# The down projection of an encoder layer: one direct pair of K-tiles instead of two ahead of the seven-product form

## The chip, the cores and the metric

The kernel runs on one core of a Trainium2 chip. The metric is device time in microseconds, from the start to the end of one execution; smaller is better. The time before is the median of three runs.

## The reference, cut to what matters

The layer works on 512 tokens of width 2048 in float32. The part that the change touches is the last matrix product of the feed-forward block, with `w_down` of 5632 x 2048:

```python
h = rmsnorm(x, ffn_norm_w[l])
x = x + (jax.nn.silu(h @ w_gate[l]) * (h @ w_up[l])) @ w_down[l]
...
return rmsnorm(x, final_norm_w)
```

Before it stand the input projection, two kinds of attention and the output projection.

## The kernel before

Every float32 product is made of three matmuls in a shorter float type: each operand is split into a high part (a cast on ScalarE) and a low part (the difference, on VectorE), and high times high, high times low and low times high are summed in PSUM. The five engines run lists of instructions whose order is written out by hand; each engine works its list strictly in order. A list entry that waits holds everything behind it on that engine.

The 5632 rows of `w_down` are 44 K-tiles of 128, or 22 pairs. A column is one of four blocks of 512 output columns. Pairs are multiplied in one of two forms:

- **Direct** (`job` kind "B", run by `run_job`, L268; matmuls L304 to L306). For one pair and one column there are two half pieces of weights (`Stream.split`, cast L198, difference L199), each used on four token blocks with three matmuls 512 wide: 24 matmuls. The activations' operands come from `g_split` (L1303 to L1307 and its other branch).
- **Seven-product form** (class `Down`, L1358, on top of `Blocks`, L1121). A pair is a 2 x 2 block product done with seven products instead of eight. For one pair and one column: three sums of weights on VectorE (`sums`, L1157 to L1159), their and the weights' high parts (`split`, L1170, two casts) and low parts (L1175, two differences of 768 and 1024 columns), and 7 products x 2 token halves x 3 matmuls 256 wide (L1455 to L1457): 42 matmuls. For one pair once, a set of activations' operands is made (`operands`, L1379): four sums (L1402 to L1405), then four casts and four differences (L1414 to L1418). `make(n)` takes n steps of that generator: step one issues loads, and then each pair takes three steps (sums; the first two splits; the last two). `operands` loads a pair's activations from the scratch tensor `gd`.

The order of the stages is: gate/up (class `Feed`, L1181, in seven-product form, matmuls L1216 to L1218, 44 units of four pieces); the direct pairs 0 and 1 of `w_down`, column by column; `Down` with sixteen pairs in three chunks (2 to 7, 8 to 12, 13 to 17), each chunk through all columns; the pairs 18 and 19 direct (`later_jobs`); the pairs 20 and 21 direct, with the final norm (`finish`).

Around the joint of gate/up and the direct stage:

- `Feed.run` calls `down_start(q)` after each of the four pieces of the last unit, which begins loads and the first splits of the direct stage.
- The PSUM banks of a gate/up unit are read out by `Feed.evac` (L1222), a generator in the list `urgent`: its first step frees the unit's first bank (L1227, L1235), the second two banks, the third the last one. `run_urgent` takes one step. `run_side`, which calls it, stands in `run_job` behind every half piece but the last of a job: three times per column with four half pieces.
- There are eight PSUM banks of 512 columns. A column of the direct stage takes four from the front of the free list and returns them in `evac_down` (L1329): ScalarE scales each bank into SBUF (L1334), and GpSimd adds it to the scratch tensor `xd` by a DMA (L1336).
- `before_down(c)` runs ahead of every half piece of the direct stage, and steps the operands of `Down`, its first sums and its first split.
- The buffers `s4` (16 slots of 4 KB per partition, names b) hold raw weights and their splits, `s2` (70 slots of 2 KB, names a) the rest. SyncE issues the loads in program order and waits at a load until its slot is free.

Of the kernel before, what the change touches and what calls it, by code (L numbers as in the profile page):

```python
# [117 lines left out]
def layer(nc, tc, x, attn_norm_w, w_in, rel_table, gw_f, gb_f, gw_b, gb_b, gla_norm_w, w_out,  # L118
# [3 lines left out]
    w_gate, w_up, w_down, out = w_gate[0], w_up[0], w_down[0], out[0]  # L122
# [3 lines left out]
    with tc.manual_schedule(), \  # L126
# [6 lines left out]
        s4 = Slots(p4, N4, 1024, "b")  # L133
# [978 lines left out]
        for c in range(4):  # L1112
            j = job("B", [piece512(w_out, c * 512, k) for k in range(0, KT, 2)], list(range(KT)),
                    lambda k: mixh[k], evac_out(c), rate=1.0, start=start_out(c), before=before_out(c), limit=3)
# [176 lines left out]
        def g_load(j):  # L1291
            if j < FF // 256 and j not in graw and 2 * j not in gT and j >= state["g"]:
                state["g"] = j + 1
                graw[j] = s4.get(F32, [P, 2, 512])
                sp.dma_start(out=graw[j].t.rearrange("p f t -> p (f t)"), in_=gd[j])

        def g_split(j):
            if j in graw:
                r = graw.pop(j)
                for f in (1, 0):  # L1300
                    hi, lo = s2.get(F32R), s2.get(F32R)
                    if f:
                        act.activation(hi.t, r.t[:, f], AF.Copy, scale=-1.0)  # L1303
                        dve.scalar_tensor_tensor(lo.t, r.t[:, f], -1.0, hi.f, op0=OP.mult, op1=OP.subtract)
                    else:
                        act.copy(hi.t, r.t[:, f])
                        dve.tensor_tensor(lo.t, r.t[:, f], hi.f, op=OP.subtract)  # L1307
                    gT[2 * j + 1 - f] = (hi, lo)
                put(r)

        def down_start(q):
            if q == 0:
                g_load(0)
            if q == 1:
                st.until = down_pieces
                st.limit = 3
                st.load()
                g_load(1)
            if q == 2:
                g_split(0)  # L1320
                st.split(down_first + 2)
            if q == 3:
                dn.make(1)

        def residual(c, t, bank):
            dve.scalar_tensor_tensor(x1[c][t].t, bank.t, rstd2[:, t:t + 1], x1[c][t].t, op0=OP.mult, op1=OP.add)
# [12 lines left out]

        def before_down(c):  # L1340
            def f(i):
                if c == 0 and i == 0:
                    g_split(1)
                dn.make(1)
                if c == 3:
                    dn.load()
                    if i >= 1:
                        dn.sums(i - 1)
                    if i == 2:
                        dn.split(0)  # L1350
            return f

# [5 lines left out]
        class Down(Blocks):  # L1358
# [5 lines left out]
            def __init__(self, chunks):  # L1364
                self.chunks = chunks
                self.end = len(chunks) - 1
                cols = lambda ch: range(3, -1, -1) if ch % 2 else range(4)
                self.begin([(ch, c, q) for ch in range(len(chunks)) for c in cols(ch) for q in chunks[ch]], 1, 256)
                self.x = {}
                self.making = self.operands()  # L1370
                self.late = []
                self.stored = set()
                self.m, self.y = {}, {}
                self.ops = deque()
# [4 lines left out]
            def operands(self):  # L1379
                a, z = slice(0, 256), slice(256, 512)  # L1380
                tt = dve.tensor_tensor
                qs = deque(q for ch in self.chunks for q in ch)
                raws = deque()

                def load():
                    if qs and len(s4.free) > 1 and len(raws) < 2:
                        r = s4.get(F32, [P, 2, 512])
                        sp.dma_start(out=r.t.rearrange("p f t -> p (f t)"), in_=gd[qs[0]])
                        raws.append((qs.popleft(), r))

                load()
                load()
                yield
                while raws or qs:
                    load()
                    if not raws or len(s2.free) < 9 + 1:
                        yield
                        continue
                    q, r = raws.popleft()
                    n1, f2 = r.t[:, 1], r.t[:, 0]  # L1400
                    t13, t24 = s2.get(), s2.get()
                    tt(t13.t[:, a], n1[:, z], n1[:, a], op=OP.subtract)  # L1402
                    tt(t13.t[:, z], f2[:, z], n1[:, z], op=OP.add)
                    tt(t24.t[:, a], f2[:, z], t13.t[:, a], op=OP.add)
                    tt(t24.t[:, z], t24.t[:, a], f2[:, a], op=OP.subtract)  # L1405
                    yield
                    todo, slots = [], []
                    for src, n in ((n1[:, a], 256), (f2, 512), (t13.t, 512), (t24.t, 512)):
                        sl, hi, lo, hf = half_split(src, n)
                        slots += sl  # L1410
                        todo.append((src, hi, lo, hf))
                    for i, (src, hi, lo, hf) in enumerate(todo):
                        if i == 0:
                            act.activation(hi, src, AF.Copy, scale=-1.0)  # L1414
                            dve.scalar_tensor_tensor(lo, src, -1.0, hf, op0=OP.mult, op1=OP.subtract)
                        else:
                            act.copy(hi, src)
                            tt(lo, src, hf, op=OP.subtract)  # L1418
                        if i:
                            put((r, t13, t24)[i - 1])  # L1420
                        if i == 1:
                            load()
                        if i % 2:
                            yield
                    (_, b1h, b1l, _), (_, f2h, f2l, _), (_, t13h, t13l, _), (_, t24h, t24l, _) = todo
                    self.x[q] = dict(slots=slots, B11=(b1h, b1l), B21=(f2h[:, a], f2l[:, a]),
                                     B22=(f2h[:, z], f2l[:, z]), T1=(t13h[:, a], t13l[:, a]),
                                     T3=(t13h[:, z], t13l[:, z]), T2=(t24h[:, a], t24l[:, a]),
                                     T4=(t24h[:, z], t24l[:, z]))
# [104 lines left out]
            def run(self):  # L1534
                for i, (ch, c, q) in enumerate(self.seq):
                    self.load()
                    self.sums(i)
                    self.split(i)
                    self.sums(i + 1)
                    self.sums(i + 2)  # L1540
                    self.split(i + 1)
                    self.evac_late(i)
                    while q not in self.x:
                        self.make(1)
                    self.products(i)
                    if c == (0 if ch % 2 else 3) or i % 3:
                        self.make(1)
                    run_urgent()
                    if ch == self.end:
                        n = self.chunks[ch].index(q)  # L1550
                        self.combine(i, 2)
                        if c == 2 and n:
                            self.fetch(3, range(2 * n - 2, min(2 * n, 7)), sp)
                        if c == 3:
                            if n == 0:
                                g_load(LAST // 2 - 2)
                            if n == 1:
                                st.until, st.limit = None, 1
                                st.load()
                            if n == 2:  # L1560
                                g_split(LAST // 2 - 2)
                                g_load(LAST // 2 - 1)
                                st.limit = 2
                                st.load()
                            if n > 2:
                                st.split(later_first + n - 2)
                self.evac_late(len(self.seq))
                st.limit, st.big = 3, tail_first
# [26 lines left out]
        st.until = len(st.pieces)  # L1595
        down_first = len(st.halves)
        for c in range(4):
            j = job("B", [piece512(w_down, c * 512, k) for k in (0, 2)], list(range(4)),
                    lambda k: gT[k], evac_down(c), before=before_down(c))
            if c == 3:  # L1600
                j.drop = drop_g
# [9 lines left out]
            if c == 3:  # L1611
                j.drop = drop_g
        tail_first = len(st.halves)
        dn = Down([list(range(2, 8)), list(range(8, 13)), list(range(13, 18))])

        wf = []

# [127 lines left out]
```

## Time and profile before

| what | value |
|---|---|
| median of three runs | 2215.56 us (2215.52 to 2216.87) |
| the profiled execution's own time | 2216.53 us |
| its span, first to last instruction | 2214.8 us |
| granted TensorE clock, mean | 0.999 |
| busy: TensorE, VectorE, ScalarE, GpSimd | 2204.3, 1623.5, 1003.0, 96.0 us |
| matmuls | 14842 |

Durations in a timeline are those of one instruction until its result stands; the next one on the same engine may start some 0.1 us before that. So the price of an instruction in a chain is taken here from start to start. TensorE's line names its weight loads (PEld) apart from its matmuls (PE).

### The profile page before, as it was taken

What the parts mean: (1) busy time and instruction counts of PE and PEld (TensorE: products, weight loads), DVE (VectorE), ACT (ScalarE), POOL (GpSimd) and SP (SyncE); (2) the same over time, 40 slices, a digit from 0 to 9 for tenths busy, and PEclk for the clock granted to TensorE, in tenths of its full rate; (3) what the DMA queues carried; (4) which work ended last, traced back from release to release, by engine and by line L of the source; (5) the groups of instructions that cost most, each with busy time, mean ns of one, the idle gap of its engine ahead of it and who ended that gap; (6) DMA issues with size and microseconds to landing.
All of it is one profiled execution on the core that took longest, in us unless ns stands there. A gap on an engine that the chain in (4) does not pass through costs nothing.

```text
span 2214.8 us, 37040 instructions
## 1 busy us (share of the span) xinstructions
PE 2204.3 (100%) x14842; PEld 2040.1 (92%) x14842; DVE 1623.5 (73%) x2740; ACT 1003.0 (45%) x1664; POOL 96.0 (4%) x149
## 2 busy tenths in 40 slices
PE   9999999999999999999999999999999999999998
PEld 7888888888888888999999999999999999999987
DVE  4366665745454438988888888888888888888795
ACT  5244444444444345444434343444343465565462
POOL 0000000000000100000000000000000010011300
PEclk9999999999999999999999999999999999999999
DMA  6525625231324332334334333343333775575982
GB/s 207 162 82 158 169 87 141 76 124 57 96 67 153 131 127 77 115 115 124 115 115 124 115 124 115 115 125 115 115 125 115 249 164 179 167 195 143 288 316 76
DMA packets 210185, 302.26 MB, mean 136 GB/s; under 512 B 15005, under 2 KB 133197, under 8 KB 210014
## 3 DMA queue, kind: packets, MB, share of 16 engines
q1 hardware_dynamic: 194366, 258.87, 37.3%
q0 software_dynamic: 15328, 40.51, 7.2%
q8 instruction: 116, 1.90, 0.4%
q10 hardware_dynamic: 320, 0.53, 0.1%
q14 instruction: 55, 0.45, 0.1%
HBM read 246.58 MB, written 40.70 MB: 130 GB/s over the span
## 4 chain that ended last, share of the span: by engine, by line
PE 99%; DVE 1%; DMA 0%; SPq 0%; ACT 0%; issue 0%; DVEq 0%
PE ps L1217 13%; PE ps L1216 13%; PE ps L1218 13%; PE ps L304 7%; PE ps L306 7%; PE ps L305 7%; PE ps L297 5%; PE ps L295 5%; PE ps L296 5%; PE ps L1457 5%; PE ps L1456 5%; PE ps L1455 5%; PE ps L532 1%; PE ps L872 1%; PE ps L541 1%; PE ps L540 1%
## 5 line engine op out<-in xcount | busy, mean ns | idle before, releaser
L1216 PE MATMUL ps<-a,b 128*128 128x256 f32 x2464 | 697.5, 283 | 0.0
L1217 PE MATMUL ps<-a,b 128*128 128x256 f32 x2464 | 697.3, 283 | 0.0
L1218 PE MATMUL ps<-a,b 128*128 128x256 f32 x2464 | 697.3, 283 | 0.0
L1170 ACT CAST b<-b 128x1024 fp32r<-128x1024 f32 (+1 forms) x473 | 438.7, 941 | 529.1 <-DVE b L1175 280.6
L1175 DVE TENSOR_TENSOR b<-b,b 128x1024 fp32r<-128x1024 f32 (+1 forms) x473 | 501.5, 1087 | 123.3 <-PE ps L1217 61.6
L1217 PEld LDWEIGHTS ps<-a,b 128*128 128x128 f32 x2464 | 473.1, 192 | 0.0
L1216 PEld LDWEIGHTS ps<-a,b 128*128 128x128 f32 x2464 | 473.1, 192 | 0.0
L1218 PEld LDWEIGHTS ps<-a,b 128*128 128x128 f32 x2464 | 473.1, 192 | 0.0
L199 DVE TENSOR_TENSOR a<-b,a 128x512 fp32r<-128x512 f32 x292 | 194.7, 686 | 132.6 <-ACT a L198 121.5
L1456 PE MATMUL ps<-b,a 128*128 128x256 f32 x896 | 253.6, 283 | 0.0
L1457 PE MATMUL ps<-b,a 128*128 128x256 f32 x896 | 253.6, 283 | 0.0
L1455 PE MATMUL ps<-b,a 128*128 128x256 f32 x896 | 253.6, 283 | 0.0
L198 ACT CAST a<-b 128x512 fp32r<-128x512 f32 x292 | 170.8, 618 | 31.9 <-DMA b<-in_w_in_dram 10.9
L304 PE MATMUL ps<-a,a 128*128 128x512 f32 x464 | 182.7, 394 | 0.0
L305 PE MATMUL ps<-a,a 128*128 128x512 f32 x464 | 180.8, 390 | 0.0
L306 PE MATMUL ps<-a,a 128*128 128x512 f32 x464 | 180.7, 390 | 0.0
L1455 PEld LDWEIGHTS ps<-b,a 128*128 128x128 f32 x896 | 172.0, 192 | 0.0
L1456 PEld LDWEIGHTS ps<-b,a 128*128 128x128 f32 x896 | 172.0, 192 | 0.0
L1457 PEld LDWEIGHTS ps<-b,a 128*128 128x128 f32 x896 | 172.0, 192 | 0.0
L1157 DVE TENSOR_TENSOR b<-b 128x512 f32<-128x512 f32 x233 | 159.5, 684 | 10.8 <-DMA b<-in_w_down_dram 10.8
L295 PE MATMUL ps<-a,a 128*128 128x512 f32 x416 | 167.3, 402 | 0.0
L297 PE MATMUL ps<-a,a 128*128 128x512 f32 x416 | 163.0, 392 | 0.1
(240 smaller groups left out, 3059.7 us busy)
## 6 DMA issues: line engine op xcount, KB each, us to landing
b<-in_w_gate_dram SPq DMA_DIRECT2D x88, 512.0 KB, 3.5
b<-in_w_up_dram SPq DMA_DIRECT2D x88, 512.0 KB, 3.9
b<-in_w_down_dram SPq DMA_DIRECT2D x88, 512.0 KB, 4.9
b<-in_w_in_dram SPq DMA_DIRECT2D x48, 512.0 KB, 4.0
b<-in_w_in_dram SPq DMA_DIRECT2D x92, 256.0 KB, 4.4
b<-in_w_out_dram SPq DMA_DIRECT2D x32, 512.0 KB, 5.5
a<-a SPq DMA_DIRECT2D x96, 128.0 KB, 2.3
gd<-b POOLq DMA_DIRECT2D x22, 512.0 KB, 3.2
```

The costliest lines, as they stand in the source:

```text
L295: mm(o, wh.t[:, c], xh.t, start=first, stop=False)
L304: mm(o, xh.t[:, c], wh.t[:, w], start=first and not on, stop=False, skip_group_check=on)
L305: mm(o, xh.t[:, c], wl.t[:, w], start=False, stop=False, skip_group_check=on)
L306: mm(o, xl.t[:, c], wh.t[:, w], start=False, stop=last, skip_group_check=on)
L1170: act.copy(o, src)
L1175: dve.tensor_tensor(o, src, h, op=OP.subtract)
L1216: mm(o, wh, xh, start=head, stop=False, skip_group_check=True)
L1217: mm(o, wh, xl, start=False, stop=False, skip_group_check=True)
L1218: mm(o, wl, xh, start=False, stop=end, skip_group_check=True)
L1455: mm(o, xh[:, t], wh, start=first and h == 0, stop=False, skip_group_check=True)
L1456: mm(o, xh[:, t], wl, start=False, stop=False, skip_group_check=True)
L1457: mm(o, xl[:, t], wh, start=False, stop=last, skip_group_check=True)
```

## The change

One direct pair goes first instead of two; pair 1 joins the first chunk of `Down`, whose chunks are now 1 to 6, 7 to 12 and 13 to 17, so seventeen pairs are in seven-product form. `down_start` no longer loads and splits pair 1 for the direct form, but steps the generator of `Down`'s operands (0, 1, 2 and 3 steps after the four pieces of the last gate/up unit). In the direct stage a column now has two half pieces; `before_down` takes two operand steps per column, loads and sums the first weights of `Down` in the columns 2 and 3, and splits the first block in the last half piece. A new field `keep` sets how many `s4` slots the operand loads leave free (4 during gate/up, 1 after). In the first column of `Down` an operand step is taken at every block rather than at two of three.

```diff
             if q == 1:
                 ...
                 st.load()
-                g_load(1)
             if q == 2:
                 g_split(0)
                 st.split(down_first + 2)
-            if q == 3:
-                dn.make(1)
+            dn.make(q)
...
         def before_down(c):
             def f(i):
-                if c == 0 and i == 0:
-                    g_split(1)
-                dn.make(1)
+                dn.keep = 1
+                if i == 0:
+                    dn.make(2)
+                if c == 2:
+                    dn.load()
+                    if i == 1:
+                        dn.sums(0)
                 if c == 3:
                     dn.load()
-                    if i >= 1:
-                        dn.sums(i - 1)
-                    if i == 2:
+                    dn.sums(1 + i)
+                    if i == 1:
                         dn.split(0)
...
+                self.keep = 4
...
-                    if qs and len(s4.free) > 1 and len(raws) < 2:
+                    if qs and len(s4.free) > self.keep and len(raws) < 2:
...
-                    if c == (0 if ch % 2 else 3) or i % 3:
+                    if c == (0 if ch % 2 else 3) or ch + c == 0 or i % 3:
                         self.make(1)
...
-            j = job("B", [piece512(w_down, c * 512, k) for k in (0, 2)], list(range(4)),
+            j = job("B", [piece512(w_down, c * 512, 0)], list(range(2)),
                     lambda k: gT[k], evac_down(c), before=before_down(c))
...
-        dn = Down([list(range(2, 8)), list(range(8, 13)), list(range(13, 18))])
+        dn = Down([list(range(1, 7)), list(range(7, 13)), list(range(13, 18))])
```

## The prediction

> **What bounds the kernel now.** I read the busy shares first, then TensorE's waits, then the timelines of TensorE, VectorE and ScalarE around the joint of gate/up and `w_down`. The page and the list of TensorE's waits over the whole span:
>
> ```profile
> PE 2204.3 (100%) x14842; PEld 2040.1 (92%) x14842; DVE 1623.5 (73%) x2740; ACT 1003.0 (45%) x1664; POOL 96.0 (4%) x149
> ```
> ```profile
> PE ps L907 <- DVE warm L388: 1.1, 1, 1.1
> PE ps L346 <- DMA b<-in_x_dram: 0.4, 1, 0.4
> ```
>
> TensorE waits 1.5 us in all, both times at the start. From there to the tail it never runs dry, so the time is the sum of its matmuls. Fewer of them is a gain, and any wait the change makes is paid in full. VectorE (DVE), at 73%, is the nearest other limit. The stages' borders, in TensorE's timeline:
>
> ```profile
> 1752.43 0.40 PE L304 MATMUL ps<-a,a 128*128 128x512 f32 x1
> ...
> 1795.97 0.28 PE L1455 MATMUL ps<-b,a 128*128 128x256 f32 x1
> ...
> 2118.53 0.40 PE L304 MATMUL ps<-a,a 128*128 128x512 f32 x1
> ```
>
> The direct stage takes 43.54 us for 2 pairs x 4 columns x 24 = 192 matmuls: 0.2268 us each. The seven-product stage takes 322.56 us for 16 x 4 x 42 = 2688 matmuls: 0.1200 us each.
>
> **The change part by part: TensorE.** Removed: 4 x 24 = 96 matmuls of 512 columns, 96 x 0.2268 = 21.77 us. Added: 4 x 42 = 168 of 256, 168 x 0.1200 = 20.16 us. The gain is 1.61 us if TensorE stays fed. The Trainium skill (TensorE: Matmul & The Clock Gate, section Back-to-back issue gap) puts an isolated matmul at N/2.4 + 2.5 ns; estimated from it the gain would be 20.72 - 18.34 = 2.4 us and the time 0.8 us lower. The rows above show 11 ns more per matmul than that rule at both widths, so they decide.
>
> **VectorE's work.** Pair 1 in direct form costs eight differences (L199) and two in `g_split`; in seven-product form it costs four times sums and low parts, and one set of operands. Prices, from VectorE's timeline around the joint:
>
> ```profile
> 1747.80 1.29 DVE L1253 TENSOR_TENSOR b<-b,a 128x512 f32<-128x512 f32 x2
> 1750.73 0.69 DVE L1304 SCALAR_TENSOR_TENSOR a<-b,a 128x512 fp32r<-128x512 f32 x1 [1.65 <-ACT a L1303]
> ...
> 1751.94 0.42 DVE L1402 TENSOR_TENSOR a<-b 128x256 f32<-128x256 f32 x1
> ...
> 1753.41 0.69 DVE L199 TENSOR_TENSOR a<-b,a 128x512 fp32r<-128x512 f32 x1
> 1754.01 0.42 DVE L1227 TENSOR_TENSOR b<-ps,a 128x256 f32<-128x256 f32 x1
> ...
> 1754.67 0.42 DVE L1415 SCALAR_TENSOR_TENSOR a<-b,a 128x256 fp32r<-128x256 f32 x1
> 1755.01 0.68 DVE L1418 TENSOR_TENSOR a<-b,a 128x512 fp32r<-128x512 f32 x1
> 1755.61 0.68 DVE L199 TENSOR_TENSOR a<-b,a 128x512 fp32r<-128x512 f32 x1
> 1756.21 0.68 DVE L1227 TENSOR_TENSOR a<-ps,a 128x512 f32<-128x512 f32 x1
> ...
> 1757.87 1.28 DVE L1418 TENSOR_TENSOR a<-a,a 128x512 fp32r<-128x512 f32 x2
> 1759.07 0.69 DVE L199 TENSOR_TENSOR a<-b,a 128x512 fp32r<-128x512 f32 x1
> 1759.67 1.22 DVE L1257 TENSOR_TENSOR b<-b,b 128x1024 f32<-128x1024 f32 x1
> 1760.81 0.42 DVE L1402 TENSOR_TENSOR a<-b 128x256 f32<-128x256 f32 x1
> ...
> 1764.56 0.43 DVE L1415 SCALAR_TENSOR_TENSOR a<-b,a 128x256 fp32r<-128x256 f32 x1 [1.60 <-ACT a L1414]
> ...
> 1775.64 1.29 DVE L1418 TENSOR_TENSOR a<-a,a 128x512 fp32r<-128x512 f32 x2 [3.86 <-ACT a L1417]
> ...
> 1786.65 0.69 DVE L199 TENSOR_TENSOR a<-b,a 128x512 fp32r<-128x512 f32 x1 [2.23 <-ACT a L198]
> ...
> 1791.53 0.68 DVE L1157 TENSOR_TENSOR b<-b 128x512 f32<-128x512 f32 x1
> ...
> 1793.05 2.08 DVE L1175 TENSOR_TENSOR b<-b,b 128x768 fp32r<-128x768 f32 x2
> 1795.05 0.42 DVE L1402 TENSOR_TENSOR a<-b 128x256 f32<-128x256 f32 x1
> ```
>
> Start to start: one L199 0.60 (1759.07 to 1759.67); an operand's four sums 1.47 (1751.94 to 1753.41), its first two low parts 0.34 + 0.60 = 0.94 (L1415, L1418), its last two 1.20 (L1418 x2), so 3.61 per pair; reading out the last gate/up unit 0.66 + 1.66, its gate product L1257 1.14; three sums of weights 1.52 (1791.53 to 1793.05); both low parts of a block 2.00, the first of them alone 0.955 by the group further below. Pair 1 moves from 10 x 0.60 = 6.0 us to 4 x (1.52 + 2.00) + 3.61 = 17.7 us. Over the whole stage that has cover:
>
> ```profile
> 1752.30:1795.80 43.50, 43.50 (x195) 36.03 (x194) 35.38 (x71) 27.32 (x50) 11.82 (x15) 1.00 0.89 231
> 1795.80:2118.50 322.70, 322.70 (x2690) 322.66 (x2689) 275.40 (x423) 175.28 (x248) 45.45 (x60) 1.00 0.70 202
> ```
> ```profile
> L1175 DVE TENSOR_TENSOR b<-b,b 128x768 fp32r<-128x768 f32 x63 | 60.1, 955 | 15.5 <-ACT b L1170 9.4 <-PE ps L1456 5.8 <-PE ps L1457 0.3
> ```
>
> VectorE (the third busy column) is idle for 47 us in the 323 of the seven-product stage. At the joint there is no such cover: the direct stage is where VectorE, at 35.4 of 43.5 us, gets ahead of TensorE, and it shrinks by 21.77 us.
>
> **First wait: the second direct column.** In the built program TensorE's second column starts on the first bank of gate/up's last unit, which L1227 and L1235 must have read; in the order of VectorE's list, operands of the pairs 1, 2 and 3 now stand ahead of them. Step by step: up to 1747.80 the list is the same. Then pair 1's sums and first low parts come in, 1.47 + 0.94 = 2.41 us, so L1253 starts at 1750.21. ScalarE's table step waits for L1253, and the casts wait behind it:
>
> ```profile
> 1749.12 1.06 ACT L1254 ACTIVATE b<-b 128x1024 f32<-128x1024 f32 x1 [2.83 <-DVE b L1253]
> 1750.08 0.61 ACT L1303 ACTIVATE a<-b 128x512 fp32r<-128x512 f32 x1
> ...
> 1761.49 2.73 ACT L1334 ACTIVATE a<-ps,small 128x512 f32<-128x512 f32 x4 [6.06 <-PE ps L306]
> 1764.12 0.41 ACT L1414 ACTIVATE a<-b 128x256 fp32r<-128x256 f32 x1
> ```
>
> So VectorE resumes at 1750.73 + 2.41 = 1753.14. Ahead of L1227 stand: pair 1's last two low parts 1.20, pair 2 whole 3.61, pair 3's sums 1.47, one L199 0.60; together 6.88. L1227 starts at 1760.02 and ends at 1760.44. TensorE would begin the column at 1752.43 + 24 x 0.2268 = 1757.87: a wait of 2.6 us. Before, the same read ended at 1754.43 and the second column began at 1752.43 + 48 x 0.2268 = 1763.3: 8.9 us of slack. On a restart a weight load may stand free:
>
> ```profile
> L1217 PEld LDWEIGHTS ps<-a,b 128*128 128x128 f32 x2464 | 473.1, 192 | 0.0
> ```
>
> I take 0 to 0.19 us for it, per wait, 0.1 as value.
>
> **Second wait: the first block of `Down`.** Its second matmul needs the low part of 768 columns. VectorE's list from L1227 at 1760.02 to there: read-out 0.66 + 1.66 + 1.14 = 3.46; five L199, 3.00; pair 3's four low parts 2.14; pair 4 whole 3.61; pair 5's sums 1.47; three sums of weights 4.56; the low part 0.955. Sum 19.2, so 1779.2 with no idle. One dependence adds to it: pair 4's last two casts stand behind the third column's read-out on ScalarE. Before, ScalarE went on 0.81 us behind a column's last matmul (1764.12 against 1763.31); the third column now ends at 1760.6 + 2 x 5.44 = 1771.5, the first cast starts at 1772.3, and VectorE gets it at about 1773.0, where its own list arrives at 1772.6. That makes 1779.6. TensorE is due at that matmul at 1752.43 + 21.77 + 0.12 = 1774.3. The two waits together are thus 5.3 us, whatever the first one is, since VectorE's list sets the second.
>
> A balance from the other side: VectorE's idle between 1743 and 1794 was 1.65 + 1.60 + 3.86 + 2.23 = 9.3 us (the four idle times in the rows above), of which 1.65 + 0.4 stay; its first low part ended at 1794.0, 2.1 us ahead of need; the work up to there shrinks by 8 x 0.60 (L199), 1.20 (`g_split`) and 2.14 (the second half of one more operand), and grows by 1.52 (one more sum): 6.6 us less. Lost time is 21.77 - 6.6 - 7.3 - 2.1 = 5.8 us. I take 5.5 us.
>
> Afterwards VectorE has about 1.5 us in hand per block: the next low parts end at 1779.6 + 0.9 + 2.0 = 1782.7, due at 1784.4. In the first column a block costs 3.52 + an operand step of 0.94 to 1.47, against 5.04 us of TensorE; later columns are as before.
>
> **Loads and queues.** The count of loads stays: four weight pieces of pair 1 move from the direct loader to `Down`'s, and one load from `gd` from `g_load` to the operands. SyncE may wait longer for slots, but the blocks that it holds back are due after 1784. GpSimd's additions into `xd` now come every 5.4 us and take 3.5 us a column; nobody waits for them near the joint. Cost nothing, with one exception under the rivals.
>
> **Sum.** -1.61 + 5.5 = +3.9 us. The profiled execution's own 2216.53 becomes 2220.4; the median stood 0.97 us lower, so 2215.56 + 3.9 = 2219.5 us.
>
> **The rivals.** *VectorE keeps up* (chance 0.12): no wait, the gain of 1.61 us stays, 2213.95 us, not slower than before. For it: not one wait of TensorE in 2200 us, and VectorE is only 73% busy. Against it: L1227 would have to end by 1757.9 rather than 1760.4, and the first low part by 1774.3 rather than 1779.6; it decides where VectorE finds 5 us of its list shorter than the rows above.
>
> *The first operands arrive late* (0.20). Pair 1's activations, whose load is issued at 1739.58, are now needed at about 1746.2 on ScalarE and 1747.8 on VectorE, rather than at 1750.1:
>
> ```profile
> 1739.58 0.34 SPq L1295 DMA_DIRECT2D b<-gd  x1
> ...
> L1295 SPq DMA_DIRECT2D b<-gd x6: 320/339/742, 1732.5 to 2129.0; - x6
> ...
> DMA to landing us min/median/max: 8.9/9.8/10.7
> ...
> 1740.00:1744.00 4.00, 4.00 (x35) 4.00 (x35) 1.88 (x4) 1.57 (x2) 0.00 (x0) 1.00 1.03 398
> ```
>
> If the load takes these 8.9 to 10.7 us it lands between 1748.5 and 1750.3 and holds VectorE for 0.7 to 2.5 us, all of it passed on: 2220.2 to 2222.0. Against it: the loads queued with it are 2 MB, at 398 GB/s some 5 us.
>
> *The first column of `Down` runs short again* (0.08): one more pair of low parts late, 2.0 us, 2221.5.
>
> *The clock drops in a wait* (0.08). After TensorE's last matmul the granted clock held for 5 us and more:
>
> ```profile
> 2205.63 0.28 PE L1649 MATMUL ps<-a,a 128*128 128x256 f32 x1
> ...
> 2210.00:2211.00 1.00, 0.00 (x0) 0.00 (x0) 0.00 (x0) 0.00 (x0) 0.00 (x0) 1.00 1.00 371
> 2211.00:2212.00 1.00, 0.00 (x0) 0.00 (x0) 0.00 (x0) 0.00 (x0) 0.00 (x0) 0.56 1.09 344
> ```
>
> By these rows waits of 2.6 us leave it alone. If it fell to half, and stayed there for as long again as it takes to fall, a wait would cost 2.7 us more: 2222.2, with both 2224.9. The Trainium skill (TensorE: Matmul & The Clock Gate, Part 1: The HAM clock gate) has it fall after one idle window of about 3.4 us; by that rule too these waits are short of it, by less.
>
> **How the numbers follow.** Forecast 0.52, rivals 0.12, 0.20, 0.08, 0.08. What this kernel's measurement can tell from no change is about 0.2%, 4.4 us: slower means over 2220.0. The forecast's own spread is 2218.6 to 2220.6 (5.3 to 5.8 us of waits, 0 to 0.4 of restarts, 0.5 for chains read from rows); 0.3 of it lies over that line, with nearly all of the three slower rivals: 0.47 slower. Same 0.50, from the rest and the first rival; faster by 4.4 us is out of reach of a gain of 1.61, 0.03 for what I have not seen. The range 2216.5 to 2222.5 leaves out the first rival and the clock in both waits.
>
> **What would show it.** Right: two waits of TensorE, for VectorE at L1227 (about 2.6 us, some 5.4 us into the direct stage) and at L1175 (about 2.8 us, at `Down`'s first block); `Down` starting near 1779.5 or, with its first matmul ahead of the wait, near 1777; the clock at 1.00; 72 matmuls more. Wrong: no waits; a wait of VectorE or ScalarE for `gd`; more waits deeper in `Down`.

## The result and the profile after

The changed kernel takes 2226.78 us (median of four runs, 2223.66 to 2227.67); the kernel before took 2215.55 us beside it. The ratio is 1.0047, with an interval of 1.0029 to 1.0064: slower by 0.5%, and above the predicted range. The profiled execution took 2226.76 us with a span of 2225.0 us, 10.2 us more than the span before. The medians differ by 11.2 us, since the profiled execution before lay 1.0 us above its median.

The busy engines, from the page of the changed kernel:

```profile
PE 2206.5 (99%) x14914; PEld 2044.8 (92%) x14914; DVE 1634.3 (73%) x2758; ACT 1006.7 (45%) x1666; POOL 96.0 (4%) x149
```

There are 72 matmuls more, as planned. The view of TensorE's waits (us in total, times, longest) has two lines that the kernel before had not:

```profile
PE ps L1458 <- DVE b L1175: 5.6, 3, 2.5
PE ps L304 <- DVE b L1227: 2.4, 1, 2.4
```

L1458 is the line that was L1456 before. One wait at L304 and one of the three at L1458 were foreseen; the other two were not. TensorE's timeline shows where they are (start, duration, in brackets the idle time before and its releaser):

```profile
1752.26 0.40 PE L304 MATMUL ps<-a,a 128*128 128x512 f32 x1
...
1757.50 0.39 PE L306 MATMUL ps<-a,a 128*128 128x512 f32 x1
1760.31 0.80 PE L304 MATMUL ps<-a,a 128*128 128x512 f32 x1 [2.42 <-DVE b L1227]
1760.90 0.63 PE L305 MATMUL ps<-a,a 128*128 128x512 f32 x1
1761.33 0.63 PE L306 MATMUL ps<-a,a 128*128 128x512 f32 x1
...
1778.31 0.28 PE L1457 MATMUL ps<-b,a 128*128 128x256 f32 x1
1781.08 0.58 PE L1458 MATMUL ps<-b,a 128*128 128x256 f32 x1 [2.50 <-DVE b L1175]
...
2004.14 0.28 PE L1457 MATMUL ps<-b,a 128*128 128x256 f32 x1
2006.82 0.39 PE L1458 MATMUL ps<-b,a 128*128 128x256 f32 x1 [2.40 <-DVE b L1175]
...
2012.84 0.39 PE L1458 MATMUL ps<-b,a 128*128 128x256 f32 x1 [0.73 <-DVE b L1175]
...
2128.74 0.40 PE L304 MATMUL ps<-a,a 128*128 128x512 f32 x1
```

Behind the first wait the matmuls follow each other by 0.43 us, not 0.2268. The table of windows shows why (length, busy us of TensorE's matmuls, of its weight loads, of VectorE, ScalarE and GpSimd; then the granted clock, the DMA share and GB/s):

```profile
1758.00:1760.00 2.00, 0.00 (x0) 0.00 (x0) 1.97 (x6) 2.00 (x5) 1.43 (x3) 1.00 0.56 218
1760.00:1761.00 1.00, 0.69 (x2) 0.60 (x3) 1.00 (x3) 1.00 (x3) 1.00 (x3) 0.61 1.11 109
1761.00:1763.00 2.00, 2.00 (x6) 1.57 (x5) 2.00 (x5) 1.88 (x4) 1.14 (x2) 0.50 1.09 155
1763.00:1764.00 1.00, 1.00 (x4) 0.80 (x3) 1.00 (x3) 0.00 (x0) 0.00 (x0) 0.68 1.04 119
1764.00:1766.00 2.00, 2.00 (x10) 1.66 (x9) 1.97 (x4) 0.41 (x1) 0.00 (x0) 1.00 1.04 180
...
1780.00:1781.00 1.00, 0.00 (x0) 0.00 (x0) 1.00 (x3) 0.97 (x2) 0.64 (x2) 0.85 1.12 203
1781.00:1784.00 3.00, 2.92 (x13) 2.92 (x14) 3.00 (x4) 0.91 (x3) 0.33 (x1) 0.50 1.13 205
...
2007.00:2009.00 2.00, 2.00 (x18) 2.00 (x19) 1.24 (x2) 1.56 (x3) 0.00 (x0) 1.00 0.55 200
```

The granted clock fell to half for 3.4 us behind the first and the second wait (0.61 in the microsecond from 1760 to 1761 is 0.78 us at half, so from 1760.22 on; likewise from 1780.70), and not behind the third.

The 10.2 us split up by the stages' borders. The direct stage takes 1778.31 - 1752.26 = 26.05 us against 96 x 0.2268 = 21.77: 4.28 more, of which 1760.31 - 1757.50 - 0.23 = 2.58 are the first wait and 1.7 the half clock. `Down` takes 2128.74 - 1778.31 = 350.4 us against 2856 x 0.1200 = 342.7: 7.7 more. Of these the second wait is 1781.08 - 1778.31 - 0.12 = 2.65, the half clock behind it about 1.5, and some 3.5 us are left for the third wait, which comes twice (2.40 and 0.73, and a restart after each). With the gain: -1.6 + 4.3 + 7.7 = +10.4, against 10.2.

Where the third wait comes from stands in the lists of VectorE, ScalarE and GpSimd of the changed kernel:

```profile
1991.05 3.54 POOL L1493 DMA_DIRECT2D md<-a  x4 [22.18 <-ACT a L1490]
...
1998.73 0.59 ACT L1490 COPY a<-ps 128x512 f32<-128x512 f32 x1 [2.45 <-DMA md<-a]
...
2000.91 0.43 DVE L1404 TENSOR_TENSOR a<-b 128x256 f32<-128x256 f32 x1 [4.35 <-DMA md<-a]
...
2003.49 0.42 DVE L1406 TENSOR_TENSOR a<-b,a 128x256 f32<-128x256 f32 x1 [1.82 <-DMA md<-a]
...
md<-a POOLq DMA_DIRECT2D x35, 256.0 KB, 9.7
```

VectorE stands 4.35 and 1.82 us at an operand step (L1404, L1406; L1402 and L1404 before). The step writes into buffers from which a column's seven results are still being added into the scratch tensor `md`; such a DMA lands 9.7 us after its issue (median). In the kernel before, GpSimd issued that column's additions from 1989.51 and 1994.57 on, and the next operand's sums came later and started with no idle time before them:

```profile
1994.57 2.65 POOL L1491 DMA_DIRECT2D md<-a  x3 [1.51 <-ACT a L1486]
...
2005.16 0.42 DVE L1402 TENSOR_TENSOR a<-b 128x256 f32<-128x256 f32 x1
```

### The profile page after: what moved, and what is told of

It is laid out like the page before. It is cut to its first block, busy times and chain, and to the rows that moved or that the text cites. A ratio compares the mean times of both kernels' runs of the same rounds, so it can differ in the third digit from the quotient of the medians.

```text
span 2225.0 us, 37209 instructions
## 1 busy us (share of the span) xinstructions
PE 2206.5 (99%) x14914; PEld 2044.8 (92%) x14914; DVE 1634.3 (73%) x2758; ACT 1006.7 (45%) x1666; POOL 96.0 (4%) x149
## 4 chain that ended last, share of the span: by engine, by line
PE 91%; issue 5%; DVE 2%; DMA 1%; ACT 0%; POOL 0%; SPq 0%; DVEq 0%; POOLq 0%; ACTq 0%
PE ps L1217 13%; PE ps L1216 13%; PE ps L1218 13%; PE ps L304 6%; PE ps L305 6%; PE ps L306 6%; PE ps L297 5%; PE ps L295 5%; PE ps L296 5%; PE ps L1458 3%; PE ps L1459 3%; PE ps L1457 3%; PE ps L532 1%; PE ps L872 1%; PE ps L541 1%
## 5 line engine op out<-in xcount | busy, mean ns | idle before, releaser
L1170 ACT CAST b<-b 128x1024 fp32r<-128x1024 f32 (+1 forms) x481 | 445.8, 941 | 536.2 <-DVE b L1175 287.7
L1175 DVE TENSOR_TENSOR b<-b,b 128x1024 fp32r<-128x1024 f32 (+1 forms) x481 | 509.8, 1087 | 123.6 <-PE ps L1217 63.2
L199 DVE TENSOR_TENSOR a<-b,a 128x512 fp32r<-128x512 f32 x284 | 189.2, 686 | 130.1 <-ACT a L198 120.6
L1458 PE MATMUL ps<-b,a 128*128 128x256 f32 x952 | 270.4, 284 | 5.6 <-DVE b L1175 5.6
L1459 PE MATMUL ps<-b,a 128*128 128x256 f32 x952 | 270.0, 284 | 0.0
L1457 PE MATMUL ps<-b,a 128*128 128x256 f32 x952 | 269.9, 284 | 0.0
L1458 PEld LDWEIGHTS ps<-b,a 128*128 128x128 f32 x952 | 183.4, 193 | 6.3 <-DVE b L1175 6.3
L1459 PEld LDWEIGHTS ps<-b,a 128*128 128x128 f32 x952 | 183.5, 193 | 0.0
L1457 PEld LDWEIGHTS ps<-b,a 128*128 128x128 f32 x952 | 183.4, 193 | 0.0
L198 ACT CAST a<-b 128x512 fp32r<-128x512 f32 x284 | 166.0, 618 | 32.7 <-DMA b<-in_w_in_dram 10.9
L304 PE MATMUL ps<-a,a 128*128 128x512 f32 x432 | 171.1, 396 | 2.4 <-DVE b L1227 2.4
L1157 DVE TENSOR_TENSOR b<-b 128x512 f32<-128x512 f32 x237 | 162.2, 684 | 10.1 <-DMA b<-in_w_down_dram 10.1
L305 PE MATMUL ps<-a,a 128*128 128x512 f32 x432 | 168.9, 391 | 0.0
L306 PE MATMUL ps<-a,a 128*128 128x512 f32 x432 | 168.8, 391 | 0.0
L295 PE MATMUL ps<-a,a 128*128 128x512 f32 x416 | 167.3, 402 | 0.0
L297 PE MATMUL ps<-a,a 128*128 128x512 f32 x416 | 163.0, 392 | 0.1
```

The lines of the kernel that those rows point to most:

```text
L295: mm(o, wh.t[:, c], xh.t, start=first, stop=False)
L304: mm(o, xh.t[:, c], wh.t[:, w], start=first and not on, stop=False, skip_group_check=on)
L305: mm(o, xh.t[:, c], wl.t[:, w], start=False, stop=False, skip_group_check=on)
L306: mm(o, xl.t[:, c], wh.t[:, w], start=False, stop=last, skip_group_check=on)
L1170: act.copy(o, src)
L1175: dve.tensor_tensor(o, src, h, op=OP.subtract)
```

## The experiments

Times are medians, beside runs of the kernel before on the same chip: 2215.92 us for the first four kernels, 2216.3 for the next four, 2216.25 for the three after them and 2216.05 for the last. Edits are against the changed kernel, but for `e5_two_early`, which starts from the kernel before, and for `e8_respread_gp` and `e11_respread_pool`, which build on `e7_respread`. Where an edit adds lines, the line numbers behind it shift by a few.

**Each wait undone alone.** `e1_chunks656` gives the second chunk back its five pairs:

```diff
-        dn = Down([list(range(1, 7)), list(range(7, 13)), list(range(13, 18))])
+        dn = Down([list(range(1, 7)), list(range(7, 12)), list(range(12, 18))])
```

> The changed kernel with the chunks 1 to 6, 7 to 11 and 12 to 17 (six, five, six pairs instead of six, six, five); nothing else. Theory (read from the trace after): the waits at 2004 and 2012 us, 3.1 us of matmul waits and some 0.4 of restarts, come from one operand step that reuses the buffer of a result whose accumulating DMA into md is still running, because the second chunk's length put the step one block behind the read-out of seven banks. With other lengths the step falls elsewhere: some 3.5 us less than the changed kernel's 2226.8, so about 2223.3, with the two waits at the joint left as they are. Rival (VectorE has too much work with seventeen pairs, and any chunk of six runs short): the wait moves to another place and the time stays at 2226 to 2227.5.

Measured: 2223.73 us, ratio 1.0034 (1.0022 to 1.0046). The third wait is gone, the other two stand at 2.4 and 2.5 us, with half clock behind each. So the third wait is worth 3 us, and it came from the regrouped chunks.

`e2_evac_first` puts the reading of the bank ahead of three operand steps:

```diff
-            dn.make(q)
+            if q < 3:
+                dn.make(q)
...
+                if c == 0 and i == 0:
+                    run_urgent()
+                    dn.make(3)
```

> The changed kernel with the first step of gate/up's last read-out ahead of the operand steps (three of the operand steps move behind it into the first direct column). Theory: the first wait (2.6 us) and the slow clock behind it (1.5 us) go, but Down's first low part stands where VectorE's list ends, near 1780 us, so the second wait grows by nearly as much: 2225 to 2226.8, the first block's wait 5 to 7 us. Rival (the two waits are independent): 4 us less, 2222.8, the wait at Down's first block 2.5 us as before.

Measured: 2224.64 us, 1.0040 (1.0027 to 1.0053). TensorE's waits:

```profile
PE ps L1462 <- DVE b L1175: 4.4, 2, 2.5
PE ps L305 <- DVE a L199: 2.3, 1, 2.3
PE ps L907 <- DVE warm L388: 1.1, 1, 1.1
PE ps L304 <- DVE b L1227: 0.4, 1, 0.4
```

A miss for both theories. The second column now starts without a wait, but 2.3 us came up one matmul later, for the low part of the column's weights (L199), which also stood behind the operand steps, and 0.4 us at the column's second bank, which a later step of the read-out frees. The wait at `Down`'s first block stays at 2.5 us, as the rival had it (the 4.4 us at L1462 are this wait and the third one). The list as a whole was late, not one entry of it.

`e3_split_first` puts the first block's split ahead of the second block's sums and leaves the third block's sums to `Down` itself:

```diff
                 if c == 3:
                     dn.load()
-                    dn.sums(1 + i)
-                    if i == 1:
+                    if i == 0:
                         dn.split(0)
+                    else:
+                        dn.sums(1)
```

> The changed kernel with the first block of Down split ahead of the second and third blocks' sums (two sums, 3.04 us, leave VectorE's list ahead of the first low part). Theory: the wait at Down's first block (2.7 us) and the slow clock behind it (1.3 us) go: about 2222.8, the first wait stays at 2.4 us with its slow clock. Rival (the wait only moves to the second block of Down, whose sums are now late): 2225 to 2226.8 with a wait at the second block.

Measured: 2222.16 us, 1.0027 (1.0017 to 1.0036). The second wait is gone; the first (2.4 us) and the third (1.9 us, at L1459) are left. In this profile the clock was at half behind the third wait too, 0.50 in 2003 to 2005.

`e4_combo` has all three edits.

> All three edits together. Theory: no wait at the second direct column, none in the chunk transitions; the list ahead of Down's first low part is 3.0 us shorter than after the change and TensorE is due there at 1774.3, so a wait of 2 to 3 us stays, with or without a slow clock of 1.3 us behind it: 2216 to 2218. Rival (waits independent, each edit takes its own away): 2214 to 2214.5.

Measured: 2218.21 us, 1.0010 (1.0000 to 1.0019). One large wait is left, the 2.3 us at L305 that `e2_evac_first` had brought out, and in this profile the clock stayed at 1.00 behind it. The theory had a wait of that size left, but at `Down`'s first block; it stands in the second direct column instead, with 0.4 us more at that column's second bank. The rival (each edit takes its own wait away, 2214.5 at most) falls.

**Halving and early start apart.** `e5_two_early` is the kernel before, with two direct pairs, and takes only the early operand steps:

```diff
-            if q == 3:
-                dn.make(1)
+            dn.make(q)
...
+                dn.keep = 1
```

> The kernel before, with its two direct pairs, but with the operand steps of gate/up's last unit as the changed kernel has them (0, 1, 2 and 3 of them in its quarters instead of one in the last). Theory (the moved steps make the first wait, by standing in VectorE's list ahead of what the direct stage needs next, and no queue or load has part in it; from then on two pairs give VectorE time enough): one wait of 1.5 to 2.5 us in the first column of the direct stage, at its second pair's weights, for a low part (L199), and none after it; the chunks are those of before, so no third wait. Time 2215.5 + 2.0 = 2217.5, or 2219 if the clock halves behind it. Rival (the halving alone makes the waits, since its columns are 5.4 us long instead of 10.9): no wait, 2215.5.

Measured: 2222.49 us, 1.0026 (1.0015 to 1.0037). TensorE's timeline, both waits in the first column:

```profile
1759.61 0.50 PE L304 MATMUL ps<-a,a 128*128 128x512 f32 x1 [1.46 <-ACT a L198]
...
1762.38 0.79 PE L305 MATMUL ps<-a,a 128*128 128x512 f32 x1 [2.27 <-DVE a L199]
```

The place is the theory's, the size not: 3.7 us of waits instead of 2, since the high part (L198, on ScalarE) was late too, and half clock from 1760.6 to 1767.4, twice as long as behind a single wait. The rival falls: the early steps alone cost the kernel before more than 6 us.

`e6_one_late` halves the direct stage and leaves the early steps out:

```diff
-            dn.make(q)
+            if q == 3:
+                dn.make(1)
```

> The changed kernel with the halving but without the early start: one operand step in the last quarter of gate/up's last unit, as before the change; the steps that are left out run in the direct stage. Theory (six steps of 17.7 us in all on VectorE must end before Down's first low parts, and the direct stage of 21.8 us is too short for them beside its own work of splits and read-outs): no wait in the direct stage, but waits of 2 to 4 us in each of Down's first three or four columns, 9 to 12 us together, and the third wait as in the changed kernel (3.5). Time 2215.5 - 1.6 + 10.5 + 3.5 = 2228, up to 2232 with halved clocks behind the waits. Rival (VectorE makes up for the late steps as the columns go on, and the early start is what costs): faster than the changed kernel's 2226.8 by two or more, 2222 to 2224.

Measured: 2234.33 us, 1.0078 (1.0064 to 1.0092). TensorE's waits, all of them in `Down`:

```profile
PE ps L1459 <- DVE b L1175: 4.7, 2, 2.8
PE ps L1458 <- ACT a L1420: 4.5, 3, 1.5
PE ps L1460 <- DVE a L1421: 2.8, 3, 0.9
```

10.1 us of waits in `Down`, as much as expected (9 to 12), but not spread over three or four columns: all of them lie in the first, at its first, fourth, fifth and sixth pair. There is a third wait of 1.9 us rather than 3.5, and the three stretches of half clock in this profile, 6.8, 3.4 and 3.4 us long, make up the rest. So the halved stage does need the early steps, and VectorE catches up by itself only after a whole column of `Down`.

**The order of the list.** `e7_respread` keeps the halving and the arithmetic and moves steps only: four of them in gate/up's last unit, the bank's read and the second column's split ahead of the others.

```diff
-            dn.make(q)
+            dn.make([1, 2, 1, 0][q])
...
+                if c == 0 and i == 0:
+                    for _ in range(2):
+                        run_urgent()
+                    st.split(down_first + 4)
+                dn.make([3, 2, 0, 2, 0, 2, 0, 0][2 * c + i])
...
+                if 2 * c + i == 5:
+                    dn.sums(0)
+                if 2 * c + i == 6:
+                    dn.split(0)
+                if 2 * c + i == 7:
+                    dn.sums(1)
+                    dn.make(2)
...
+        dn = Down([list(range(1, 7)), list(range(7, 12)), list(range(12, 18))])
```

> The halving kept, its steps put elsewhere, all arithmetic the same: four steps in the last unit (1, 2, 1, 0 by quarters), the read of the last unit's bank and the second column's weight split ahead of the steps of the direct stage, the steps spread over its eight quarters, the first sum of the first column ahead of its split and the second behind it, chunks of 6, 5 and 6 pairs. Theory (all three waits are places in VectorE's list, and with the list in due order only VectorE's lack of time is left): waits of 0.8 us at most each, 1.5 us together, all in the direct stage; none in Down; no halved clock. Time 2215.5 - 1.6 + 1.5 = 2215.4. Rival (VectorE's work doesn't fit in any order, so that the wait shows at another place, over 2 us): 2217.5 or more, as in the run with all three parts undone.

Measured: 2215.9 us against 2216.3, 0.9998 (0.9989 to 1.0006), span 2214.4. What is left of the waits stands in two rows:

```profile
1763.69 0.50 PE L305 MATMUL ps<-a,a 128*128 128x512 f32 x1 [0.58 <-DVE a L199]
...
1766.96 0.50 PE L305 MATMUL ps<-a,a 128*128 128x512 f32 x1 [0.22 <-DVE a L199]
```

The theory holds: all three waits, and the half clock with them, came of places in VectorE's list. It is no measurable gain over the kernel before: the direct stage takes 23.21 us (1751.82 to 1775.03) against 21.77, so what is left of the waits, with the restarts behind them, uses up nearly all of the 1.61 us.

`e8_respread_gp` gives the last unit's product of gate and up to GpSimd and spreads the steps in ones; `e11_respread_pool` does the first of these alone:

```diff
-                    dve.tensor_tensor(c_.t, c_.t, self.gate.t, op=OP.mult)
+                    (pool if j == FF // 256 - 1 else dve).tensor_tensor(c_.t, c_.t, self.gate.t, op=OP.mult)
```

> As the run before, with one of VectorE's operations in that stretch, the product of the last unit's gate and up (L1257, 1.22 us), done by GpSimd, and the steps of the direct stage in ones instead of twos. Theory (VectorE lacks about 1.5 us there; this gives 1.2 of it back, and GpSimd is idle in that stretch): one wait of 0.4 us or none, time 2215.5 - 1.6 + 0.4 = 2214.3. Rival (GpSimd works slower than VectorE and the product comes later to the store and the load of the last pair's gate, or slows VectorE while it runs): VectorE's operations beside it over 1.3 times as long as in the run before, and the waits of that run stay: 2215.4 or more.

> The run with the steps respread (2215.9 against 2216.3 of before) with one edit alone: the product of the last unit's gate and up on GpSimd, as in the run after it, but the steps of the direct stage as in that of the respread ones. It parts the two edits of the GpSimd run, whose wait of 1.0 us was for a high part on ScalarE. Theory (that wait came of the steps in ones, which put ScalarE's casts of an operand ahead of the second column's weights; GpSimd's 2.7 us disturb nothing): VectorE's freed 1.2 us take away the waits of 0.58 and 0.22 us, none over 0.9 left, 2215.9 - 0.5 = 2215.4. Rival (GpSimd's product is what cost there): waits of 1 us or more in the direct stage, 2217.

Measured: 2217.35 us, 1.0004 (0.9995 to 1.0013), and 2218.37 us, 1.0009 (1.0000 to 1.0018). Both show a wait of 1.0 us at L304 for a high part, and one of 0.6 and 0.8 us in `Down`, where `e7_respread` had none. The theory of `e11_respread_pool` (the wait comes of the steps in ones) falls; its rival is right, and so is that of `e8_respread_gp`. VectorE and GpSimd in `e11_respread_pool`:

```profile
1754.89 3.48 DVE L199 TENSOR_TENSOR a<-b,a 128x512 fp32r<-128x512 f32 x2
1755.11 2.71 POOL L1257 TENSOR_TENSOR b<-b,b 128x1024 f32<-128x1024 f32 x1 [28.75 <-DVE b L1227]
```

Two L199 take 3.48 us beside GpSimd's product (in `e8_respread_gp` too), against 1.28 in `e7_respread`: VectorE loses 2.2 us for the 1.2 that it was spared.

**The clock.** `e9_filled` is the changed kernel with zeros multiplied and added into a bank of the first and of the fourth direct column, which changes nothing in their sums, at the places where TensorE would run dry. `e12_filled_656` has 11 of them per place instead of 18, and the chunks of `e1_chunks656`.

```diff
+                            if j.fill and last and b == 3:
+                                for _ in range(j.fill):
+                                    mm(o[:, 0:P], warm, warm, start=False, stop=False)
...
+            j.fill = 18 if c in (0, 3) else 0
```

> The changed kernel with TensorE kept busy where it waits: 18 matmuls of 128x128 with zeros as both operands, added into the last bank of the first and of the fourth direct column ahead of their last three matmuls. By the 128x128 float32 matmuls elsewhere in the trace (0.13 us each) they take 2.3 us, as long as the first and the second wait. VectorE's list, the loads and every read-out but that of those two banks stay as they are, so what TensorE waits for comes no sooner. Theory (idle time of TensorE brings the half clock behind these two waits, 1.4 us each): waits of 0.2 us in place of 2.4 and 2.5, no half clock in 1760 to 1785, third wait as before: 2226.8 - 2.8 = 2224.0. Rival (the half clock comes of something else in that stretch, such as the DMA traffic or the load on the other engines, or on a clock of its own): the matmuls behind the filled waits still take 0.43 and 0.21 us, time 2226.8.

Measured: 2225.41 us, 1.0042 (1.0030 to 1.0055). The clock stayed at 1.00 from 1752 to 1790. The filling was too long: 36 matmul records and 3.94 us per place (1757.36 to 1761.30), where 2.3 were meant, which uses up most of what the clock gave back. The third wait did not stay as it was: it is 1.20 and 1.41 us here.

> As the filled run, with two changes: 11 pairs of zero matmuls in each place instead of 18, since there a matmul of 128x128 in float32 was two records of 0.11 us and the 18 took 3.94 us instead of 2.3, and the chunks of 6, 5 and 6 pairs, which take the third wait away. So it stands against the run with these chunks alone (2223.73, 2222.38 to 2224.24 in 6 runs, ratio 1.0034), which has both waits with half clock behind each in its profile. Theory (the half clock comes of TensorE's idle time): 11 times 0.219 is 2.4 us, as long as each wait; no half clock in 1750 to 1790, no wait over 0.5, time 2223.7 - 2 x 1.4 = 2220.9, and the runs within 1 us of each other, since it is the half clock that comes or stays away from run to run. Rival (the clock drops there whatever TensorE does): half clock in the profile behind one place or both, 2223.7, spread 2 us as there.

Measured: 2219.73 us, 1.0017 (1.0008 to 1.0026), eleven runs from 2219.26 to 2220.88; `e1_chunks656` ran from 2222.38 to 2224.24. A place's filling in TensorE's timeline:

```profile
1774.82 0.39 PE L310 MATMUL ps<-a,a 128*128 128x512 f32 x1
1775.05 2.62 PE L307 MATMUL ps<-warm 128*128 128x128 f32 x22
1777.42 0.48 PE L308 MATMUL ps<-a,a 128*128 128x512 f32 x1
```

and the window over both places (the clock is the third number from the end):

```profile
1752.00:1785.00 33.00, 32.92 (x192) 28.65 (x191) 31.85 (x61) 25.54 (x44) 14.63 (x17) 1.00 1.06 239
```

TensorE is as late as with the waits (2.37 us of filling at each place), its operands come no sooner, and yet the kernel is 4 us quicker than with the same chunks and idle waits. So the half clock comes of TensorE's idle time. The runs spread over 1.6 us where 1 was expected, and 1.9 in `e1_chunks656`, so the spread does not come from the clock alone. The gain of 4.0 us is more than the expected 2.8; two whole stretches of half clock account for 3.4, and the rest is open.

**The third wait.** `e10_step_later` keeps the chunks of 6, 6 and 5 and leaves two operand steps out where a column's results are being added into `md`, so that the generator goes on two pairs later:

```diff
-                    if c == (0 if ch % 2 else 3) or ch + c == 0 or i % 3:
+                    if (ch, c) == (1, 0):
+                        self.make([0, 0, 1, 1, 1, 1][q - 7])
+                    elif c == (0 if ch % 2 else 3) or ch + c == 0 or i % 3:
                         self.make(1)
```

> The changed kernel, its chunks of 6, 6 and 5 kept, but with the operand steps of the first two pairs in the second chunk's last column (pairs 7 and 8) left out there, so that the generator's next step comes two pairs (10 us) later, where the results of the column before have been added into md. Theory (it is not the chunk's length but the step's place behind the read-out that makes the third wait: the step takes buffers that the adding DMAs still read): third wait gone, the first two waits as they are, 2226.8 - 3.3 = 2223.5. Rival (the longer chunk leaves too few buffers or too little of VectorE's time wherever the step stands): a wait of 2 us or more in 1990 to 2050 or at the third chunk's start, 2226 or more.

Measured: 2222.41 us, 1.0028 (1.0018 to 1.0038). TensorE's waits are 2.5 us for L1175 and 2.4 us for L1227, once each, and the granted clock is 1.00 through the first of them (1750 to 1779) and at half behind the second; the third is gone, and the moved step starts in VectorE's list without idle time before it:

```profile
2004.44 0.42 DVE L1404 TENSOR_TENSOR a<-b 128x256 f32<-128x256 f32 x1
```

So it is the step's place behind the read-out, not the chunk's length or the number of buffers.

## Why the prediction was wrong

**TensorE's gain of 1.61 us: right.** In `e12_filled_656`, where no wait is left, `Down` takes 343.05 us (1778.20 to 2121.25) for its 2856 matmuls, 0.1201 us each. The gain and 2 x 2.37 us of filling make -1.6 + 4.7 = +3.1 us; measured are +2.7 by the spans and +3.7 by the medians, so the runs show the gain to within some 0.6 us.

**First wait: right in place, cause and size.** L1227 was to begin at 1760.02 and did at 1759.84; 2.6 us predicted, 2.42 idle and 2.58 from start to start measured.

**Second wait: right in VectorE's list; that the sum fits is luck.** The two together were to be 5.3 us; they are 2.58 + 2.65 = 5.2. But two shifts of nearly the same size cancel in that. The half clock brought TensorE 1.7 us later to the second wait, and the low part began 1.5 us later than predicted (1780.08 against 1778.6). VectorE stood twice for casts that ScalarE's list has behind a column's read-out, and the second column, at half clock, ended late (ScalarE's and VectorE's rows of the changed kernel):

```profile
1765.59 2.73 ACT L1332 ACTIVATE a<-ps,small 128x512 f32<-128x512 f32 x4 [2.70 <-PE ps L306]
...
1768.65 0.42 DVE L1417 SCALAR_TENSOR_TENSOR a<-b,a 128x256 fp32r<-128x256 f32 x1 [1.00 <-ACT a L1416]
...
1774.36 1.29 DVE L1420 TENSOR_TENSOR a<-a,a 128x512 fp32r<-128x512 f32 x2 [0.64 <-ACT a L1419]
...
1780.08 4.09 DVE L1175 TENSOR_TENSOR b<-b,b 128x768 fp32r<-128x768 f32 x4
```

The prediction had 0.4 us for the second of these idle times and nothing for the first. In `e12_filled_656`, where the clock holds, VectorE has neither, and its list takes the time that was predicted: from L1253 (there L1257) to the low part (there L1179) 28.6 us, against 28.4 predicted (1750.21 to 1778.6) and 30.05 in the changed kernel (1750.03 to 1780.08):

```profile
1748.98 1.29 DVE L1257 TENSOR_TENSOR b<-b,a 128x512 f32<-128x512 f32 x2
...
1777.55 2.09 DVE L1179 TENSOR_TENSOR b<-b,b 128x768 fp32r<-128x768 f32 x2
```

**"Later columns are as before": the first step that failed, 3.5 us (3.1 by `e1_chunks656`).** The prediction counted what VectorE has to do in a column and not which buffers its steps write. With six pairs in the second chunk and a step at every block of a chunk's last column, the steps fell right behind a read-out. The same holds for "Loads and queues … Cost nothing": it followed the loads, and not the DMAs that read from the buffers to be refilled.

**"By these rows waits of 2.6 us leave it alone": the second step that failed, 3.2 us.** The rival of the clock was there, at a chance of 0.08 and a price of 2.7 us a wait; it came true at both waits, at 1.7 and 1.5 us. The rows of the span's end, where the clock held for 5 us, were read as a delay that starts with the idle time. By the last section's reading of the traces, the clock is judged in windows of 3.41 us that lie fixed in time: there the first window had 1.95 us of idle time in it, too little, and only the whole idle one behind it brought the drop. The rule of the Trainium skill that the prediction set beside it (TensorE: Matmul & The Clock Gate, Part 1: The HAM clock gate), one idle window of about 3.4 us, has the length right, and its free-running window too; but a window need not be idle as a whole, and where the page and these runs differ, the runs decide.

**The other rivals.** The operands did not come late: neither VectorE nor ScalarE waits for `gd` in the stretch. VectorE did not keep up. `Down`'s first column ran short only at its first block.

With both failed steps out of the way, as in `e12_filled_656`, the kernel stands 3.7 us above the one before; the prediction's sum was 3.9.

## What to carry to other kernels

Where an engine that had never waited is made to wait, price the wait twice: once for itself and once for what the clock may do behind it, here up to 1.7 us for each 2.4 us, or nothing, by where the wait falls; in `e6_one_late` waits of 1.5 and 0.9 us close together did it in two of three places. When a step of a hand-written order moves, ask of it not only what it waits to read but who still reads the buffers that it writes; a DMA that added results into memory held them for some 10 us here (9.7 in the median). A stage in which a second engine gets ahead can be worth more than the matmuls that it costs: here 1.61 us of TensorE's time were traded for a cover that the change then missed.

## What was not expected of the hardware

- **Half clock after waits of 2 us, by windows that lie fixed in time.** Where a profile has several drops, their starts are whole multiples of 3.413 us apart: 1760.22 and 1780.70 in the changed kernel (6.00), 1759.86 and 2002.20 in `e3_split_first` (71.0), 1775.92, 1799.82 and 1816.88 in `e6_one_late` (7.00 and 5.00). The two starts of `e3_split_first` come from these windows (the clock is the third number from the end; 0.93 means 0.14 us at half, 0.60 means 0.80):

```profile
1759.00:1760.00 1.00, 0.57 (x2) 0.53 (x3) 1.00 (x4) 1.00 (x4) 1.00 (x3) 0.93 0.94 90
...
2002.00:2003.00 1.00, 1.00 (x8) 1.00 (x7) 0.85 (x2) 0.89 (x2) 0.00 (x0) 0.60 1.05 393
```

With this grid laid over each profile that has a drop, and TensorE's idle time taken from a matmul's due end to the next one's start, a drop stands, up to the last matmul, behind every window with 2.07 us or more of idle time (twelve, from 2.07 to 2.65) and behind none with 1.96 or less (1.96, 1.88, 1.72, 1.68 are the largest). In the changed kernel the first wait has 2.49 us in one window, the second 2.27, and the third is cut in two, 1.72 and 0.84. The first wait is the same 2.4 us in four profiles: it lies in one window in the changed kernel, `e1_chunks656` and `e3_split_first` (2.49, 2.58 and 2.57 us) and a drop follows, and in `e10_step_later` it is cut into 1.68 and 0.89 and none does. So the same wait may or may not halve the clock, by where it falls; that between 1.96 and 2.07 us lies a threshold is a reading of these rows, and no run was made to set a wait to either side of it. A stretch lasts one window of 3.41 us where the window behind the drop has 0.38 us of idle time or less, and two (6.8 us) where it has 0.70 (`e6_one_late`) or 1.80 (`e5_two_early`).
- **GpSimd stops VectorE.** The rows of `e11_respread_pool` above: 3.48 us for two differences beside GpSimd's product instead of 1.28. The Trainium skill (SBUF — State Buffer, section Who interferes with whom) says that a VectorE instruction with two inputs in SBUF contends with a GpSimd instruction that reads SBUF; the trace agrees.
- **A 128x128 matmul of float32 zeros** (L307) left two records and took 0.22 us (18 in 3.94 us in `e9_filled`, 11 in 2.37 us in `e12_filled_656`).
